# A hybrid block on one core: gates' stores in written order on GpSimd, the copy of inverse row sums between two row maxima, and the first gated rows' sums one tile later

## Chip, core and metric

The kernel runs on one core of one Trainium2 chip. The metric is the device time of one execution in microseconds (us), as the median of several runs; lower is better. A core has TensorE (PE, the matmuls), VectorE (DVE), ScalarE (ACT), GpSimd (POOL) and SyncE (SP). Each runs its own instructions one after the other, and they meet at semaphores. Transfers between the device memory and the on-chip memory go through DMA queues. Here SP and GpSimd issue them: SP's are in the queue that the profile calls q1 and GpSimd's in q0. Matmul results land in PSUM banks, out of which DVE or ACT must move them before a bank is used again.

## What is computed

The reference is one layer of a residual block on x of 1024 rows by 1024 columns, in float32:

```python
def mixer(h, w_in, b_f, conv_w, w_branch, w_out):
    proj = jnp.einsum("bsd,dn->bsn", h, w_in)
    q, k, v, f_logit, g_b, g_c, hc, gate_conv, gate_attn = jnp.split(proj, _SPLITS, axis=-1)
    ya = g_b * causal_depthwise_conv(g_c * hc, conv_w)
    logf = jax.nn.log_sigmoid(f_logit + b_f)
    yb = forgetting_attention(q, k, v, logf)      # 8 heads of 64, causal, blocks of 128 queries
    ya_d = jnp.einsum("bsc,cd->bsd", ya, w_branch[0])
    yb_d = jnp.einsum("bsc,cd->bsd", yb, w_branch[1])
    merged = jax.nn.sigmoid(gate_conv) * ya_d + jax.nn.sigmoid(gate_attn) * yb_d
    return jnp.einsum("bsd,de->bse", merged, w_out)

def swiglu(h, w_gate_up, w_down):
    g, u = jnp.split(jnp.einsum("bsd,df->bsf", h, w_gate_up), 2, axis=-1)
    return jnp.einsum("bsf,fd->bsd", jax.nn.silu(g) * u, w_down)

h = rmsnorm(x, norm_mix_pre);  x = x + rmsnorm(mixer(h, ...), norm_mix_post)
h = rmsnorm(x, norm_ffn_pre);  x = x + rmsnorm(swiglu(h, ...), norm_ffn_post)
```

The FFN has 2816 hidden columns. The attention's softmax is divided at the end by its row sums, of which the kernel forms the inverses.

## The kernel before

**Products.** The large products are cut into two by two blocks and done with seven block products in place of eight (Strassen's scheme in Winograd's form). For that, sums S1 to S4 of the blocks of one factor and T1 to T4 of the other are formed beforehand, and the block products are added up afterwards in the accumulators `c11`, `c12`, `c21` and `c22`. Every float32 operand is cut into a high and a low part (`hi` and `lo`, names such as `hT12h` and `hT12l`), and a block product is three matmuls: low times high, high times low, high times high. In the projection and the FFN DVE and ACT cut up the weights ("raw" tiles, loaded by SP) a tile ahead of PE, DVE also adds the products up (`c<-c,b`), and ACT drains some banks.

**Order.** All instructions go through a wrapper (lines 65 to 79). An engine that is named in `strict[0]` gets its instruction pinned behind the one that was written just before it on that engine. An instruction that is not pinned is placed by the scheduler: among those that are ready by its reckoning, the one written earlier goes first. Pinning fixes the order of issue alone; the waits for data are the same.

**The projection.** Eighteen jobs run one after the other: 0 to 3 for q and k, then the parts of the short convolution, and 10 to 17 for the gates. Each is one `strassen` call of some 84 matmuls. A gate job ends with the sigmoids of its four accumulators on ACT and four stores of 256 KB to `sg_dram` by GpSimd (lines 1291 to 1295). In the job 17, the last, the attention has already begun, its order is wholly written out (`last_pair`), and no sigmoid is taken. Beside the jobs, other work is spread in small steps over the additions of the `strassen` calls (table `plans`): the operands of the branch product (`ya_steps`, which loads `rows` from `ya_dram`, and stores blocks to `ya_ops`) and of the output product (`wo_steps`, which loads `r` and `l` from `w_out` and stores to `wt_dram`). These steps are pinned on DVE and GpSimd.

**The attention.** Twenty-one steps t; in each PE forms the scores of up to two blocks of rows for a pair of heads, DVE takes the row maximum of each head (`row_max`, which also writes the scores into the on-chip memory), ACT the exponentials, and PE the products with v. All engines are in written order here. At the steps 8, 13, 17 and 19 `inverse_rows` takes the inverse of a pair's row sums on DVE (`ri`), transposes it on PE (`tr`), and returns a function, `turned`, which copies the transpose (`rT<-tr`, DVE), stores it to the device memory and has SP load it back spread over the partitions. The step loop calls `turned` behind the row maxima of the first group; at t = 17, the third pair's, it calls it ahead of them (lines 1641 to 1643).

**The FFN.** Twenty-two hidden tiles of 128 columns, f = 0 to 21, each one `strassen` call. The first product of the first ten is formed ahead, so such a tile takes PE about 13.6 us; f = 2 stands at about 757.6 to 771.2 us and f = 3 up to 785. A tile ends with the gated rows `yf` (`um<-sgf,c`, DVE), two halves of one slot of `um`. For the down product their Winograd sums are formed from two tiles at a time by the generator `y_sums(k)`, k = f // 2. Its first half stores A12 and A22 and forms and stores S1 and S3; its second forms and stores S2 and S4 (`um<-um` on DVE, one `a_dram` store each on GpSimd). Before the change the first half runs at an odd f, the second at the next f (lines 2286 to 2291). The sums and their stores aren't pinned.

## Time and profile before

| what | us |
|---|---|
| median of 3 runs | 1310.73 (1310.16 to 1311.96) |
| profiled execution | 1313.74 |
| its span, first to last instruction | 1312.0 |
| TensorE busy | 1301.8 (99%), 6671 matmuls |
| VectorE busy | 948.5 (72%) |
| ScalarE busy | 564.0 (43%) |
| GpSimd busy | 207.8 (16%) |
| DMA | 235.64 MB, 180 GB/s on average |

The profile comes from one execution, whose time is 1.7 us longer than its span. Each line of a timeline names the start, the duration, the engine, the operation with the written tile, an arrow and the tiles read, and in square brackets how long the engine had been idle before and what ended that. Since nearly all instructions go through one helper, all have the line L76, and they are told apart by tiles. The stages stand in this order: the first norm and the start of the products with it up to about 63 us, the jobs of the projection to about 395, the attention from there to about 550, the rest of the branch product, the output product and the first products of ten hidden tiles to about 730, the hidden tiles to about 1096, and the down product to the end.

### The profile page before, as it was taken

How to read it: one execution, taken by the hardware profiler on the slowest of the kernel's cores; microseconds unless marked ns; L12 is line 12 of the kernel's file. 1: busy time of each engine (PE TensorE's matmuls, PEld its weight loads, DVE VectorE, ACT ScalarE, POOL GpSimd, SP SyncE). 2: the span in 40 equal slices, each digit the busy share in tenths (PEclk: the TensorE clock that was granted, in tenths of full speed). 3: DMA queues.
4: the chain of work that ended last, by engine and by line, in shares of the span. 5: the costliest groups of instructions: out<-in, count | busy, mean ns of one | idle time of the engine just before them, and what ended most of it. 6: DMA issues, size and time to landing. Idle time of an engine off the chain costs nothing.

```text
span 1312.0 us, 17799 instructions
## 1 busy us (share of the span) xinstructions
PE 1301.8 (99%) x6671; PEld 1084.2 (83%) x6671; DVE 948.5 (72%) x1361; ACT 564.0 (43%) x880; POOL 207.8 (16%) x375
## 2 busy tenths in 40 slices
PE   9999999999999999999999999999999999999998
PEld 8988888888788888888888878888888888888886
DVE  6877778776666678887677688866766666676675
ACT  6633333243355766423778332322232234444451
POOL 4101111112122222101232122111100110000000
PEclk9999999999999999999999999999999999999999
DMA  6355535557557566875486565533323337965551
GB/s 223 91 162 186 182 130 176 163 191 236 196 198 255 181 221 201 264 257 176 123 239 216 168 207 184 185 106 105 113 72 120 104 115 273 365 210 193 160 169 64
DMA packets 179639, 235.64 MB, mean 180 GB/s; under 512 B 12233, under 2 KB 121873, under 8 KB 179041
## 3 DMA queue, kind: packets, MB, share of 16 engines
q1 hardware_dynamic: 153392, 146.11, 35.5%
q0 software_dynamic: 26144, 88.40, 18.7%
q8 instruction: 52, 0.85, 0.3%
q14 instruction: 35, 0.28, 0.1%
q10 hardware_dynamic: 16, 0.00, 0.0%
HBM read 164.94 MB, written 69.53 MB: 179 GB/s over the span
## 4 chain that ended last, share of the span: by engine, by line
PE 95%; DVE 2%; DMA 2%; issue 1%; ACT 0%; SPq 0%; DVEq 0%; POOLq 0%; POOL 0%; ACTq 0%
PE b L76 60%; PE pd L76 16%; PE pv L76 4%; PE pbb L76 3%; PE pba L76 3%; PE po L76 3%; PE tps L76 3%; PE sp L76 2%; PE tp L76 1%; PE ma L76 1%; DMA raw<-in_w_in_dram 1%; PE mb L76 1%; DMA raw<-in_w_gate_up_dram 1%; DMA xt<-in_x_dram 0%; DVE c L76 0%
## 5 line engine op out<-in xcount | busy, mean ns | idle before, releaser
L76 DVE TENSOR_TENSOR c<-c,b 128x512 f32<-128x512 f32 x215 | 146.6, 683 | 72.9 <-PE b L76 70.8
L76 DVE TENSOR_TENSOR lo<-raw,hi 128x1024 fp32r<-128x1024 f32 (+1 forms) x91 | 109.7, 1205 | 73.5 <-PE b L76 57.0
L76 ACT ACTIVATE hi<-raw 128x1024 fp32r<-128x1024 f32 (+1 forms) x98 | 99.6, 1016 | 93.5 <-PE b L76 49.2
L76 ACT ACTIVATE hi<-sx 128x1024 fp32r<-128x1024 f32 x44 | 46.7, 1062 | 185.5 <-PE b L76 160.7
L76 DVE TENSOR_TENSOR lo<-sx,hi 128x1024 fp32r<-128x1024 f32 x44 | 53.8, 1223 | 38.9 <-PE b L76 37.7
L76 PE MATMUL b<-w12h,lo 128*128 128x512 f32 x208 | 80.9, 389 | 0.0
L76 DVE TENSOR_TENSOR sx<-raw 128x512 f32<-128x512 f32 x78 | 53.7, 688 | 36.9 <-DMA raw<-in_w_in_dram 25.6
L76 PE MATMUL b<-w12h,hi 128*128 128x512 f32 x204 | 79.4, 389 | 0.0
L76 PE MATMUL b<-w12l,hi 128*128 128x512 f32 x204 | 79.4, 389 | 0.0
L76 PE MATMUL b<-hh,hi 128*128 128x512 f32 x176 | 68.9, 392 | 0.5 <-DVE c L76 0.5
L76 PE MATMUL b<-hl,hi 128*128 128x512 f32 x176 | 68.5, 389 | 0.0
L76 PE MATMUL b<-hh,lo 128*128 128x512 f32 x176 | 68.5, 389 | 0.0
L76 PE MATMUL b<-w,s4h 128*128 128x512 f32 x208 | 64.1, 389 | 0.0
L76 POOL DMA_DIRECT2D a_dramA<-um x33 | 17.9, 543 | 287.4 <-DVE um L76 286.9
L76 PE MATMUL pd<-hi,lo 128*128 128x512 f32 x160 | 62.3, 389 | 0.0
L76 PE MATMUL pd<-hi 128*128 128x512 f32 x160 | 61.9, 390 | 0.0
L76 PE MATMUL pd<-ghi 128*128 128x512 f32 x148 | 57.6, 389 | 0.0
L76 PE MATMUL pd<-glo,ghi 128*128 128x512 f32 x148 | 57.6, 389 | 0.0
L76 PE MATMUL pd<-ghi,glo 128*128 128x512 f32 x148 | 57.6, 389 | 0.0
L76 PE MATMUL b<-hT12h,lo 128*128 128x512 f32 x136 | 53.0, 390 | 1.6 <-DVE lo L76 1.6
L76 ACT ACTIVATE sgf<-c 128x512 f32<-128x512 f32 x32 | 20.3, 633 | 77.8 <-DVE c L76 60.2
L76 PE MATMUL b<-hT34h,hi 128*128 128x512 f32 x136 | 53.0, 390 | 0.0
(492 smaller groups left out, 3637.7 us busy)
## 6 DMA issues: line engine op xcount, KB each, us to landing
raw<-in_w_gate_up_dram SPq DMA_DIRECT2D x52, 512.0 KB, 3.9
raw<-in_w_in_dram SPq DMA_DIRECT2D x35, 512.0 KB, 5.7
a_dramS<-um POOLq DMA_DIRECT2D x44, 256.0 KB, 3.0
a_dramA<-um POOLq DMA_DIRECT2D x33, 256.0 KB, 2.4
sg<-sg_dram SPq DMA_DIRECT2D x32, 256.0 KB, 5.5
graw<-a_dramS SPq DMA_DIRECT2D x14, 512.0 KB, 3.9
sg_dram<-c POOLq DMA_DIRECT2D x24, 256.0 KB, 2.4
raw<-in_w_down_dram SPq DMA_DIRECT2D x11, 512.0 KB, 6.0
```

What stands on the lines that cost most here:

```text
L76: ins = getattr(self.engine, name)(*args, **kw)
```

## The change

It has three parts, which touch three stages.

1. **Gate jobs** (from line 1294): GpSimd is named in `strict[0]` while the four `sg_dram` stores of a gate job are written, so they take their written place between the pinned steps of the branch and output operands. The last two are written in the other order, `c22` before `c21`.
2. **Attention, step 17** (lines 1641 to 1643): the early call of `turned` is taken out. The call behind the row maxima of the first group, which all other steps use, now copies the third pair's inverse rows as well. The first group of step 17 has one row block of one head, so the copy stands between the row maxima of the block's first head and its second.
3. **FFN** (lines 2286 to 2291): `y_sums(0)` runs its first half at f = 2 (before: f = 1) and its second at f = 3 (before: f = 2), where it stands ahead of the first half of `y_sums(1)`. The other sums stay.

```diff
                 for t in (c12, c21, c22):
                     nc.scalar.activation(t, t, AF.Sigmoid)
-            for r, c, t in ((0, n1, so), (0, n2, c12), (1, n1, c21), (1, n2, c22)):
+            strict[0] = ("gpsimd",)
+            for r, c, t in ((0, n1, so), (0, n2, c12), (1, n2, c22), (1, n1, c21)):
                 nc.gpsimd.dma_start(sg_dram[j][r, :, c], t)
+            strict[0] = ()
...
         if t <= 5:
             po_copy = pv_pair(t - 2)
-        if turned and t == 17:
-            turned()
-            turned = None
         for i, e in now[0]:
             row_max(t, i, e)
...
         if f % 2:
             late_sums = y_sums(f // 2)
+        if f == 2:
+            first_sums = late_sums
+            next(first_sums)
+        if f == 3:
+            next(first_sums)
+        if f % 2 and f > 1:
             next(late_sums)
-        else:
+        if f % 2 == 0:
             nc.gpsimd.dma_start(a_dram["A11"][f // 4][f // 2 % 2], yf[:, n1])
-        if f and (f % 2 == 0 or f == NF - 1):
+        if f > 2 and (f % 2 == 0 or f == NF - 1):
             next(late_sums)
```

## The prediction, made before the changed kernel was run

> **What bounds the kernel now.** First the page: its head and its chain of waits by engine.

> ```profile
> span 1312.0 us, 17799 instructions
> PE 1301.8 (99%) x6671; PEld 1084.2 (83%) x6671; DVE 948.5 (72%) x1361; ACT 564.0 (43%) x880; POOL 207.8 (16%) x375
> PE 95%; DVE 2%; DMA 2%; issue 1%; ACT 0%; SPq 0%; DVEq 0%; POOLq 0%; POOL 0%; ACTq 0%
> ```

> TensorE is busy for 99% of the span. The change takes no matmul away, so its gain can come only out of places where PE stands still. Next the waits of PE, and three pieces of the chain of waits in order of time.

> ```profile
> PE b L76 <- DVE lo L76: 1.6, 1, 1.6
> ...
> PE b L76 <- DVE c L76: 0.5, 1, 0.5
> PE sp L76 <- DVE nm L76: 0.3, 1, 0.3
> ...
> 323.18 9.67 DMA raw<-in_w_in_dram
> 763.11 6.60 DMA raw<-in_w_gate_up_dram
> 777.33 318.73 PE b L76 x1404
> ```

> The three waits shown are one event each, and each lies beside one part of the diff; the two left out are at the start of the kernel, before any of it. The last row gives the undisturbed pitch: 318.73 / 1404 = 0.227 us from the start of one matmul to the next. Shown idle time counts from a modelled end, so I price a stall as start to start minus the usual pitch.

> **Stall A (part 1's neighbourhood).** PE, then DVE, in the timeline:

> ```profile
> 335.51 0.39 PE L76 MATMUL b<-hT12l,hi 128*128 128x512 f32 x1
> 337.51 0.50 PE L76 MATMUL b<-hT12h,lo 128*128 128x512 f32 x1 [1.60 <-DVE lo L76]
> 332.97 0.69 DVE L76 TENSOR_TENSOR sx<-raw 128x512 f32<-128x512 f32 x1 [6.47 <-DMA raw<-in_w_in_dram]
> 336.23 1.22 DVE L76 TENSOR_TENSOR lo<-raw,hi 128x1024 fp32r<-128x1024 f32 x1
> ```

> 337.51 - 335.51 - 0.227 = 1.77 us lost. The raw weights, issued by SP at 323.18, land 9.67 us later (332.85). DVE has waited 6.47 us and then needs until 337.45 to cut the operand that PE wants. Had the transfer taken 7.9 us (332.85 - 1.77 = 331.08), nothing would be lost; each us later costs one.

> **Stall B (part 2).**

> ```profile
> 513.66 0.47 PE L76 MATMUL sp<-hi 64*128 64x448 f32 x1
> 514.43 0.44 PE L76 MATMUL sp<-hi 64*128 64x448 f32 x1 [0.30 <-DVE nm L76]
> 510.61 0.25 DVE L76 RECIPROCAL ri<-rsum 128x16 f32<-128x16 f32 x1
> 511.72 0.28 DVE L76 COPY rT<-tr 16x128 f32<-16x128 f32 x1 [0.86 <-PE tr L76]
> 511.93 1.20 DVE L76 CUSTOM_DVE_ANT_0 pt<-sp,rows 128x1024 f32<-128x1024 f32 x1
> 513.07 1.21 DVE L76 CUSTOM_DVE_ANT_0 pt<-sp,rows 128x1024 f32<-128x1024 f32 x1
> ```

> 514.43 - 513.66 = 0.77, less one pitch: 0.55 us lost. The score matmul at 514.43 needs the bank that the second row maxima read until 514.28. Both maxima stand behind the copy `rT<-tr`, which waits 0.86 us for a transpose.

> **Stall C (part 3).**

> ```profile
> 776.48 0.39 PE L76 MATMUL b<-w12h,lo 128*128 128x512 f32 x1
> 777.33 0.50 PE L76 MATMUL b<-hh,hi 128*128 128x512 f32 x1 [0.46 <-DVE c L76]
> 758.79 0.68 DVE L76 TENSOR_TENSOR um<-um 128x512 f32<-128x512 f32 x1
> 765.41 0.69 DVE L76 TENSOR_TENSOR um<-um 128x512 f32<-128x512 f32 x1
> 769.80 0.69 DVE L76 TENSOR_TENSOR sx<-raw 128x512 f32<-128x512 f32 x1 [1.95 <-DMA raw<-in_w_gate_up_dram]
> 776.60 0.68 DVE L76 TENSOR_TENSOR c<-c,b 128x512 f32<-128x512 f32 x1
> ```

> 777.33 - 776.48 - 0.227 = 0.62 us lost: the add at 776.60, which frees a bank, stands in a backlog that DVE has had since its 1.95 us wait for the raw weights at 769.80. The three `um<-um` between 758.79 and 765.41 (first and last quoted) are the sums S1, S2 and S4 of the first gated rows.

> The three stalls together are 2.94 us, 0.22% of the time. What this kernel's measurement can tell from no change is about 0.2%, 2.6 us: even all three gone would show only just.

> **The change, part by part.**

> *Part 2, the copy between two maxima.* It removes and adds no instruction. The first maxima can start where the reciprocal ends, at 510.61 + 0.25, about 510.87, and run into the time in which DVE waited. They end near 512.05; the copy, whose transpose was done at 511.72, follows, and the second maxima begin about 512.25 and end about 513.45, ahead of the score matmul's place (about 513.87). So DVE's wait of 0.86 us goes and stall B with it: -0.55. What moves besides: the copy's DMAs, the store of the inverse and SP's loads back, come 0.3 us later and serve a division steps later. Next late there is nothing: DVE is 0.83 us earlier. Bounds: 0 (if something else on DVE fills the gap) and -0.55.

> *Part 3, the sums one tile later.* Same four sums, same four `um` stores and the stores of A12 and A22; S1 and S3 go from f=1 to f=2, S2 and S4 to f=3. Each sum costs DVE 0.6 us from start to start (758.79 to the next instruction). Two of the three, S1 and S2, stand ahead of the subtraction that frees the raw buffer; its load goes out at 763.11 and takes 6.60 us. With 2 x 0.6 = 1.2 us less ahead of it the load goes out at about 761.9 and lands about 768.5; the backlog starts 1.2 us earlier, the add comes at 775.4, and PE, due at 776.71, does not wait: -0.62. The price is paid one tile on, where two sums of the first pair and two of the second meet. There S2 and S4 of the first pair, 2 x 0.6 = 1.2 us, come on top of S1 and S3 of the second. Their cover is the time in which DVE waits for PE in the tile after the stall, in the table by windows (us, then busy time of PE, PEld, DVE, ACT and POOL):

> ```profile
> 785.60:799.20 13.60, 13.60 (x62) 11.26 (x61) 11.53 (x17) 4.03 (x5) 3.78 (x7) 1.00 0.68 224
> ```

> 13.60 - 11.53 = 2.07 us are free there, more than 1.2. The stores move on GpSimd's queue only, 1.5 MB of them a tile later, and their readers are the down products, tiles later. These sums are not pinned, so the scheduler may also leave one where it was. Bounds -0.73 (the slower next pitch included) and +0.5 (the sums push the next tile's add as far as these did); taken -0.6.

> *Part 1, the gates' stores in written order.* No bytes change: four stores of 256 KB per gate job, each about 0.55 us of GpSimd. What changes is what they stand behind. GpSimd before, in the timeline, jobs 12 and 13:

> ```profile
> 309.14 0.55 POOL L76 DMA_DIRECT2D rows<-ya_dram  x1
> 312.15 0.54 POOL L76 DMA_DIRECT2D rows<-ya_dram  x1
> 314.60 0.54 POOL L76 DMA_DIRECT2D sg_dram<-c  x1 [1.91 <-ACT c L76]
> 322.24 0.72 POOL L76 DMA_DIRECT2D ya_ops<-yh  x1 [2.57 <-issue]
> 327.58 0.56 POOL L76 DMA_DIRECT2D sg_dram<-c  x1 [2.99 <-ACT c L76]
> ```

> The row at 314.60 was the last of job 12's four stores. Now these wait behind the pinned stores of the branch operand, two of 0.7 us whose data come about when that row went, so all four go at about 316 to 318. The two `rows` loads are written behind the stores and pinned, so they no longer go at 309.14 and 312.15 but near 319. That is 2 MB (4 x 256 KB and 2 x 512 KB) taken out of the stretch up to 315 and put into 316 to 332, the flight of the raw load that makes stall A. Against it one store (327.58) leaves that flight, 0.25 MB. What the load meets there is in the DMA views of 326 to 330 and of 330 to 332:

> ```profile
> q0 software_dynamic: 308, 1.13, 76.2%
> q1 hardware_dynamic: 296, 0.15, 18.3%
> ...
> q1 hardware_dynamic: 735, 0.37, 61.2%
> q0 software_dynamic: 109, 0.33, 41.0%
> ```

> While GpSimd's queue (q0) is full, SP's (q1, where the raw load is) moves 0.15 MB in 4 us, 38 KB/us; as q0 runs dry, 0.37 MB in 2 us, 185 KB/us. The 512 KB load thus ends about when q0 has drained. By total rate, (1.13 + 0.15) / 4 = 0.32 MB/us, 1.75 MB more would take 5.5 us more; but GpSimd issues the later traffic of that stretch later too (322.24 already waited 2.57 us to be issued), so that part of it falls behind 332, when the load is through. Bounds: -1.77 (the store at 327.58 and what slips are enough for the load to land by 331.08) and +5 (q0 full until the raw load has crept through). I take a fifth of the upper way, nearest to the row that shows q0 draining at 330 with 2 MB more in front and some 1.5 MB slipping behind: the load 0.7 us later, +0.7.

> [...]

> Two more places. Job 15's stores now all precede the two `wt_dram` stores behind which ACT waits in the first row below, 0.75 MB or, at 0.32 MB/us, 2.3 us more ahead of `wt_dram<-h`:

> ```profile
> 385.00 1.06 ACT L76 ACTIVATE h<-l 128x1024 fp32r<-128x1024 f32 x1 [2.73 <-DVE lo L76]
> 391.88 0.60 ACT L76 ACTIVATE c<-ma 128x512 f32<-128x512 f32 x1
> 394.35 0.39 PE L76 MATMUL ma<-hT12h,hi 128*128 128x512 f32 x1
> 411.90 0.88 POOL L76 TENSOR_TENSOR yb<-rows,mask 128x128 f32<-128x128 f32 x2
> 415.95 0.28 DVE L76 CUSTOM_DVE_ANT_0 rows<-sp,yb 128x128 f32<-128x128 f32 x1
> ```

> ACT overwrites `h` at 385.00, after that store has read it, and works through to the eviction that ends at 392.48, 1.87 us ahead of the matmul that needs the bank: at worst 2.3 - 1.87 = 0.4 us, taken 0. And job 17's four stores, 4 x 0.55 = 2.2 us, now stand ahead of the mask work at 411.90; waiting their turn they push it to about 415.2, its end to 416.05, 0.1 us into DVE's read at 415.95. DVE is not what PE waits for there: 0, at worst 0.2.

> **Sum** against the profiled execution, 1313.74 us (span 1312.0 and 1.74 around it): +0.7 - 0.55 - 0.6 = -0.45. The profiled execution is 3.0 us above the median of the runs shown (1310.73), so the forecast is that median less 0.45, 1310.3.

> **Rivals.**
> 1. *All three stalls go.* If less of the branch traffic meets the raw load, -1.77 - 0.55 - 0.62 = -2.94: 1307.8. For it: the load needs to be only 1.77 us quicker, and one 256 KB store leaves. Against it: 2 MB move towards it. Chance 0.17.
> 2. *Slower: the raw load starves.* One mechanism at 326 to 338: if q0 is never empty until the load is through, it moves its 512 KB at 38 KB/us from 326 on, with 0.06 MB or so landed before, to about 338, +5 and more; +5 - 1.15 = +3.85: 1314.6. It decides from a landing of about 334.1 on (+1.2, where the gains of parts 2 and 3 are used up), and shows as slower from 336.6 on. For it: the packets row above. Against it: GpSimd itself is held up by its waits to issue, which spaces the traffic. Chance 0.11.
> 3. *The reordering does not do what it says*: the sums, unpinned, stay at 758 to 765 and the load lands as before; only part 2 counts, -0.55: 1310.2. Chance 0.22, and not to be told from the forecast by the time alone.

> **How the numbers follow.** The forecast's case (part 1 between -1 and +3, parts 2 and 3 mostly won) has 0.50. Cases 3 and the forecast lie within 0.2% (1308.1 to 1313.35), 0.72 together. Rival 1 at 1307.8 is just over the line; a quarter of it stays within, so faster is 0.15 with 0.02 of other luck; slower is rival 2, 0.11, and 0.02 for the attention's start; same 0.72. The range goes from rival 1 with 0.2 to spare, 1307.6, to a landing 2.9 us above the forecast's, 1313.2; it leaves out rival 2 and a little of rival 1.

> **What would show it.** Stall B: the wait of `sp` for `nm` gone from PE's waits, the copy between two maxima near 512.0. Stall C: the wait on `c` at 777 gone, the raw load out by 762, and three or four `um<-um` behind 771. Part 1: in the timeline of GpSimd the `rows` loads near 319, the raw load issued at 323.18 landing between 332 and 335, and `b` still waiting for `lo` by 1 to 4 us. I am wrong if that load lands by 331, if it lands after 336, or if a wait stands at 394 or 416 that was not there.

## The result, and the profile after

The changed kernel took 1317.23 us (median of 6 runs, 1316.07 to 1319.53), the kernel before 1310.10 us beside it (6 runs, 1309.92 to 1311.96). The ratio is 1.0053, with a 95% interval of 1.0040 to 1.0066: 7 us slower, where 0.5 us faster was forecast, and above the range. The profiled execution of the changed kernel took 1317.19 us with a span of 1315.4 us.

First the waits of PE in the changed kernel (in total, times, longest, us):

```profile
PE b L76 <- DVE lo L76: 3.0, 1, 3.0
PE spin L76 <- DVE zero L76: 1.4, 1, 1.4
PE b L76 <- DVE c L76: 0.5, 1, 0.5
...
PE pba L76 <- DVE yB L76: 0.2, 1, 0.2
```

Stall B (`sp` for `nm`) is gone. Stall A has grown from 1.6 to 3.0 us. A wait for `c` of the size of stall C is still there, and the wait of `pba` for `yB` is new. Both kernels run the same 6671 matmuls, in the same order but for two that the scheduler set ahead of 36 others near 763 to 772, so the loss can be placed: take a matmul's start in the changed kernel less the start of the same matmul before, and see where this difference steps.

| place (time before) | the difference steps by | what is there |
|---|---|---|
| up to 12 us | -1.87 | the start; full clock was granted from 11.2 us on in the profiled execution of before (a `spin` matmul took 0.41 us at 9.6 and 0.28 at 11.6), from 5.2 us on in this one; no part of the change is there |
| 337.5 | +1.37 | stall A longer |
| 337.5 to 345 | +2.79 | matmuls at half clock |
| 394 to 400 | +0.67 | the matmuls on `ma` and `mb` |
| 418 | +0.87 | `pba<-yB` |
| 514 | -0.74 | stall B gone |
| 762 to 771 | +1.26 | new stalls in the FFN tile f = 2 |
| 775 to 786 | -0.95 | stall C gone |

At the last matmul the difference is 3.47 us; without the start it would be 5.3.

**Stall A.** The piece of the chain with the load, then DVE, then PE:

```profile
321.40 11.04 DMA raw<-in_w_in_dram
...
332.56 0.69 DVE L76 TENSOR_TENSOR sx<-raw 128x512 f32<-128x512 f32 x1 [7.84 <-DMA raw<-in_w_in_dram]
...
333.74 0.39 PE L76 MATMUL b<-hT12l,hi 128*128 128x512 f32 x1
337.09 0.80 PE L76 MATMUL b<-hT12h,lo 128*128 128x512 f32 x1 [2.97 <-DVE lo L76]
337.69 0.63 PE L76 MATMUL b<-hT12h,hi 128*128 128x512 f32 x1
338.11 0.63 PE L76 MATMUL b<-hT12l,hi 128*128 128x512 f32 x1
```

The raw load now takes 11.04 us (9.67 before), and the stall is 337.09 - 333.74 - 0.227 = 3.12 us. Then comes what the forecast did not have: from 337.69 the matmuls follow each other at 0.43 us in place of 0.227. The table by windows (us, busy time of PE, PEld, DVE, ACT, POOL, then the granted clock, DMA share, GB/s) names it:

```profile
333.00:337.05 4.05, 1.12 (x5) 0.58 (x4) 3.98 (x7) 1.68 (x3) 1.09 (x2) 0.91 0.07 30
337.05:341.00 3.95, 3.91 (x9) 3.17 (x10) 3.33 (x6) 1.64 (x3) 0.54 (x1) 0.50 0.98 289
341.00:345.00 4.00, 4.00 (x14) 3.17 (x14) 1.64 (x3) 2.00 (x2) 0.00 (x0) 0.73 0.65 195
```

PE is busy in the second row and does 9 matmuls in the time of 17: its granted clock is 0.50. A busy PE is not a fast one, and the waits don't show this loss at all.

**What the load meets.** GpSimd in the timeline, then the DMA view of 323 to 331, and last GpSimd's queue over the whole flight of the load, before (323.2 to 332.85) and in the changed kernel (321.4 to 332.4):

```profile
314.30 0.55 POOL L76 DMA_DIRECT2D sg_dram<-so  x1
...
316.76 0.54 POOL L76 DMA_DIRECT2D rows<-ya_dram  x1
317.71 0.54 POOL L76 DMA_DIRECT2D rows<-ya_dram  x1 [0.40 <-issue]
...
324.02 0.55 POOL L76 DMA_DIRECT2D l<-in_w_out_dram  x1 [2.24 <-issue]
...
q0 software_dynamic: 760, 2.74, 86.1%
q1 hardware_dynamic: 738, 0.38, 16.5%
...
q0 software_dynamic: 601, 2.13, 62.1%
q0 software_dynamic: 878, 3.14, 73.4%
```

Job 12's stores and the `rows` loads stand where the forecast put them (316.76 is 318.5 on the clock of before). In these 8 us of the flight GpSimd's queue moves 2.74 MB, and the raw load's queue 0.38 MB in nearly as many packets, 47 KB/us. Over the whole flight GpSimd's queue moves 3.14 MB, 1.0 MB more than before.

### The profile page after: what moved, and what is told of

The parts are those of the page before. It is cut to its first block, busy times and chain, and to the rows that moved or that the text cites. A ratio compares the mean times of both kernels' runs of the same rounds, so it can differ in the third digit from the quotient of the medians.

```text
span 1315.4 us, 17789 instructions
## 1 busy us (share of the span) xinstructions
PE 1303.2 (99%) x6671; PEld 1083.5 (82%) x6671; DVE 949.7 (72%) x1361; ACT 564.4 (43%) x880; POOL 207.7 (16%) x375
## 4 chain that ended last, share of the span: by engine, by line
PE 96%; DMA 2%; DVE 1%; issue 1%; ACT 0%; DVEq 0%; POOLq 0%; POOL 0%; ACTq 0%
PE b L76 60%; PE pd L76 16%; PE pv L76 3%; PE pbb L76 3%; PE pba L76 3%; PE tps L76 3%; PE po L76 2%; PE sp L76 2%; PE tp L76 1%; PE ma L76 1%; DMA raw<-in_w_in_dram 1%; DMA raw<-in_w_gate_up_dram 1%; PE mb L76 0%; DVE lo L76 0%; DVE sx L76 0%
## 5 line engine op out<-in xcount | busy, mean ns | idle before, releaser
L76 DVE TENSOR_TENSOR c<-c,b 128x512 f32<-128x512 f32 x215 | 146.6, 682 | 79.9 <-PE b L76 74.3
L76 DVE TENSOR_TENSOR lo<-raw,hi 128x1024 fp32r<-128x1024 f32 (+1 forms) x91 | 109.6, 1204 | 76.2 <-PE b L76 60.3
L76 ACT ACTIVATE hi<-raw 128x1024 fp32r<-128x1024 f32 (+1 forms) x98 | 99.6, 1016 | 95.3 <-PE b L76 49.4
L76 ACT ACTIVATE hi<-sx 128x1024 fp32r<-128x1024 f32 x44 | 46.7, 1062 | 199.5 <-PE b L76 171.5
L76 DVE TENSOR_TENSOR lo<-sx,hi 128x1024 fp32r<-128x1024 f32 x44 | 53.8, 1223 | 40.0 <-PE b L76 38.8
L76 PE MATMUL b<-w12h,lo 128*128 128x512 f32 x208 | 80.9, 389 | 0.0
L76 PE MATMUL b<-w12h,hi 128*128 128x512 f32 x204 | 79.4, 389 | 0.0
L76 PE MATMUL b<-w12l,hi 128*128 128x512 f32 x204 | 79.4, 389 | 0.0
L76 DVE TENSOR_TENSOR sx<-raw 128x512 f32<-128x512 f32 x78 | 53.6, 688 | 31.5 <-DMA raw<-in_w_in_dram 22.2
L76 PE MATMUL b<-hh,hi 128*128 128x512 f32 x176 | 69.0, 392 | 0.6 <-DVE c L76 0.5
L76 PE MATMUL b<-hh,lo 128*128 128x512 f32 x176 | 68.5, 389 | 0.0
L76 PE MATMUL b<-hl,hi 128*128 128x512 f32 x176 | 68.5, 389 | 0.0
L76 PE MATMUL b<-w,s4h 128*128 128x512 f32 x208 | 64.0, 389 | 0.0
L76 POOL DMA_DIRECT2D a_dramA<-um x33 | 17.9, 543 | 287.4 <-DVE um L76 287.0
L76 PE MATMUL pd<-hi,lo 128*128 128x512 f32 x160 | 62.2, 389 | 0.0
L76 PE MATMUL pd<-hi 128*128 128x512 f32 x160 | 61.9, 390 | 0.0
L76 PE MATMUL pd<-ghi 128*128 128x512 f32 x148 | 57.6, 389 | 0.0
L76 PE MATMUL pd<-glo,ghi 128*128 128x512 f32 x148 | 57.6, 389 | 0.0
L76 PE MATMUL pd<-ghi,glo 128*128 128x512 f32 x148 | 57.6, 389 | 0.0
L76 PE MATMUL b<-hT12h,lo 128*128 128x512 f32 x136 | 54.0, 397 | 3.0 <-DVE lo L76 3.0
L76 PE MATMUL b<-hT12h,hi 128*128 128x512 f32 x136 | 53.6, 394 | 0.0
L76 PE MATMUL b<-hT12l,hi 128*128 128x512 f32 x136 | 53.6, 394 | 0.0
## 6 DMA issues: line engine op xcount, KB each, us to landing
raw<-in_w_gate_up_dram SPq DMA_DIRECT2D x52, 512.0 KB, 4.0
raw<-in_w_in_dram SPq DMA_DIRECT2D x35, 512.0 KB, 5.7
graw<-a_dramS SPq DMA_DIRECT2D x14, 512.0 KB, 3.9
raw<-in_w_down_dram SPq DMA_DIRECT2D x11, 512.0 KB, 5.7
```

Of the source, the lines that this page charges most:

```text
L76: ins = getattr(self.engine, name)(*args, **kw)
```

## The experiments

Each kernel is given against the kernel before, run beside it on the same chip. The first theory, P, is that part 1 is the loss, by the load's flight, the half clock behind the stall, and smaller stalls at 394 and 418. Its rivals stand in the expectations.

### The three parts apart

Part 1 alone, parts 2 and 3 without it, part 2 alone and part 3 alone; each has the hunks of the diff above that belong to it.

> Only part 1 (gate stores in written order). Theory P: the whole loss is part 1: the raw load lands 1.6 us later, and the longer stall costs another 2.6 us of half clock behind it, 0.9 at the matmuls on ma/mb and 0.8 where the masks lie beside a DVE subtraction: 5 to 7 us above before, and a window behind the stall with a granted clock near 0.5. Rival Q: the loss comes from part 3's other order in the FFN or from the execution: within 1.5 us of before.

> Parts 2 and 3 without part 1. Theory P: about -0.2 us against before (part 2 -0.5, part 3 +0.1 to +0.4 since its stall only moves one tile ahead), no half clock anywhere. Rival Q: 3 us or more above before.

> Only part 2 (the copy between two maxima). Theory P: the 0.55 us wait of sp for nm at step 17 gone, time -0.3 to -0.6 us. Rival: something else at that place takes the gain, 0.0.

> Only part 3 (the sums one tile later). Theory P: the wait on c near 777 gone, a like one about 8 us ahead of it in its place, net 0 to +0.5 us. Rival (my forecast's step): -0.6 us.

| kernel | median, us (runs) | before, us | ratio, 95% interval |
|---|---|---|---|
| part 1 alone | 1317.06 (5) | 1311.44 (27) | 1.0050, 1.0036 to 1.0063 |
| parts 2 and 3 | 1311.40 (11) | 1311.44 | 1.0000, 0.9991 to 1.0010 |
| part 2 alone | 1310.98 (11) | 1311.44 | 0.9993, 0.9982 to 1.0005 |
| part 3 alone | 1312.46 (11) | 1311.44 | 1.0006, 0.9998 to 1.0015 |

Part 1 is the loss; Q falls. In the profile of part 2 alone the wait of `sp` for `nm` is gone, and the matmuls step 0.74 us closer there, as in the seven other profiles with part 2 (0.73 to 0.74). DVE in the changed kernel has the copy between the two maxima, without a wait:

```profile
514.68 1.16 DVE L76 CUSTOM_DVE_ANT_0 pt<-sp,rows 128x1024 f32<-128x1024 f32 x1
...
515.76 0.27 DVE L76 COPY rT<-tr 16x128 f32<-16x128 f32 x1
515.97 1.20 DVE L76 CUSTOM_DVE_ANT_0 pt<-sp,rows 128x1024 f32<-128x1024 f32 x1
```

So the copy does what was forecast, though so small a gain is inside the interval. Part 1 alone kept its full clock in the profiled execution (1.00 from 333 to 345), against the expectation, with a stall of 3.33 us; that execution, 1314.29 us, was the shortest of its five. Nor did it lose anything at 394, where P put 0.9 us.

Part 3 behaves as P has it in kind, at a higher price than its 0.5 us. In the changed kernel, DVE and PE in the timeline:

```profile
768.09 0.68 DVE L76 TENSOR_TENSOR um<-um 128x512 f32<-128x512 f32 x1
770.23 0.69 DVE L76 TENSOR_TENSOR sx<-raw 128x512 f32<-128x512 f32 x1 [1.45 <-DMA raw<-in_w_gate_up_dram]
770.84 0.68 DVE L76 TENSOR_TENSOR um<-um 128x512 f32<-128x512 f32 x1
771.44 1.22 DVE L76 TENSOR_TENSOR lo<-raw,hi 128x1024 fp32r<-128x1024 f32 x1
772.57 0.68 DVE L76 TENSOR_TENSOR c<-c,b 128x512 f32<-128x512 f32 x1
...
773.31 0.50 PE L76 MATMUL b<-hh,hi 128*128 128x512 f32 x1 [0.50 <-DVE c L76]
```

The raw load went out and landed earlier, as forecast (770.23 is about 767.0 on the clock of before, where it was 769.80). But the scheduler, which places the unpinned instructions, set `sx<-raw` of the next tile, which waits for it, ahead of `lo<-raw` and of the add at 772.57, which frees the bank for this tile's last product. Before, those two ran at 766.03 and 767.17, ahead of the wait. So stall C left 777 and came back three products (36 matmuls) earlier, at 773.31. About a third of the new loss, 0.45 of the 1.26 us, stands still earlier, from 767.03 on, behind the two matmuls that the scheduler set ahead; the profile names no wait for it. Together the new loss is 1.15 to 1.55 us in the six profiles with part 3, 1.35 on average; the old one, which is gone in all of them, took 0.03 to 0.94 in the twelve without, 0.43 on average. Part 3 so costs 0.9 us against the usual execution, and 1.0 us in the medians. S2 and S4 also still run at 768.09 and 770.84, in f = 2: written one tile later, they weren't executed a tile later.

### Which gate jobs

Part 1 for some of the jobs only; the other stores as before.

```diff
+            strict[0] = ("gpsimd",) if ij < 14 else ()     # and: in (14, 15); > 15; != 12; == 12
+            order = ((0, n1, so), (0, n2, c12), (1, n1, c21), (1, n2, c22))
+            if strict[0]:
+                order = order[:2] + order[:1:-1]
+            for r, c, t in order:
```

> Part 1 only for the gate jobs 10 to 13; the later stores unpinned as before. Theory P: the raw load issued near 322 still takes 11 us, the stall near 337 is 3.3 us, and in most executions half clock follows it for 2.6 us: 4.5 to 6 us above before. Rival R (the loss sits in the later jobs and the start of the attention): within 1.5 us of before.

> Part 1 only for jobs 14 and 15. Theory P: the store of h behind job 15's stores may reach ACT late, the matmuls on ma wait 0 to 0.9 us, no stall over 2 us near 337: 0 to +0.9 us. Rival R: +2 us or more.

> Part 1 only for jobs 16 and 17. Theory P: job 17's four stores push the mask work on GpSimd onto DVE's subtraction yB<-yraw,yB, which then takes 2.2 us in place of 1.5, and the pba matmuls wait: +0.7 us. Rival R: +2 us or more; rival S: the mask work lies beside nothing that PE waits for, 0.

> Part 1 for every gate job but 12: job 12's stores and the two rows loads stand in the order of before, all else as in part 1 alone. Theory P (the 2 MB moved at job 12 meet the raw load): flight of the raw load 5 to 9.7 us as in the kernels without part 1, stall 0 to 1.8 us, no half clock; +0.7 us stays from jobs 16 and 17: 1311 to 1312. Rival U (job 13's stores, moved too, delay it): flight 11 us and 1316 to 1317.

> Part 1 for job 12 alone (its four stores, and behind them the two rows loads). Theory P (job 12 is the whole of it): the raw load takes about 11 us, stall 3.3 us, median 5 to 6 us above before. Rival W (it takes job 13's stores as well): 2 us or less.

| part 1 for | median, us (runs) | before, us | ratio, 95% interval |
|---|---|---|---|
| jobs 10 to 13 | 1316.83 (5) | 1310.82 (23) | 1.0040, 1.0026 to 1.0053 |
| jobs 14 and 15 | 1311.11 (12) | 1310.82 | 1.0003, 0.9992 to 1.0015 |
| jobs 16 and 17 | 1311.58 (11) | 1310.82 | 1.0007, 0.9997 to 1.0016 |
| all but job 12 | 1311.81 (11) | 1310.81 (35) | 1.0008, 0.9998 to 1.0017 |
| job 12 alone | 1315.92 (7) | 1311.69 (19) | 1.0030, 1.0019 to 1.0042 |

Job 12 is enough for the long stall and its clock, and without it they are gone; R, U and W fall. Job 12 alone costs 4.2 us in the medians, less than the 5 to 6 that P gave it. For job 12 alone, PE in the timeline and two windows:

```profile
334.76 0.39 PE L76 MATMUL b<-hT12l,hi 128*128 128x512 f32 x1
338.51 0.69 PE L76 MATMUL b<-hT12h,lo 128*128 128x512 f32 x1 [3.36 <-DVE lo L76]
...
337.00:339.00 2.00, 0.49 (x1) 0.40 (x2) 2.00 (x4) 1.58 (x2) 1.10 (x2) 0.91 0.34 133
339.00:341.00 2.00, 2.00 (x6) 1.61 (x5) 1.42 (x4) 1.11 (x2) 0.54 (x1) 0.50 0.91 237
```

With jobs 16 and 17 alone PE loses 0.91 us near 418 (0.7 was expected), as in every kernel with these jobs in written order (0.87 to 0.91 us, none in the others). DVE and GpSimd there:

```profile
413.10 2.18 DVE L76 TENSOR_TENSOR yB<-yraw,yB 128x1024 fp32r<-128x1024 f32 x1
...
413.10 0.45 POOL L76 TENSOR_TENSOR yb<-rows,mask 128x128 f32<-128x128 f32 x1
413.50 0.28 POOL L76 COPY yb<-rows 128x128 f32<-128x128 f32 x1
413.75 0.45 POOL L76 TENSOR_TENSOR yb<-rows,mask 128x128 f32<-128x128 f32 x1
414.16 1.43 POOL L76 TENSOR_TENSOR rows<-rows,mask 128x128 f32<-128x128 f32 x1
```

And before, the same subtraction, the one mask beside it, and the next subtraction of the same form:

```profile
416.16 1.50 DVE L76 TENSOR_TENSOR yB<-yraw,yB 128x1024 fp32r<-128x1024 f32 x1
416.12 0.45 POOL L76 TENSOR_TENSOR rows<-rows,mask 128x128 f32<-128x128 f32 x1 [1.11 <-DVE nm L76]
...
421.70 1.22 DVE L76 TENSOR_TENSOR yB<-yraw,yB 128x1024 fp32r<-128x1024 f32 x1
```

Before, all mask work but one instruction was done when the subtraction started; it took 1.50 us, and 1.22 with no mask beside it. Beside four instructions of the mask work DVE takes 2.18 us, and the last mask 1.43 in place of 0.46. Side by side both engines' instructions grow, DVE's by 0.96 us and the mask by 0.97; how they hold each other up, no run here shows. In time, 0.8 us is inside the interval; S is refuted by the profiles. With jobs 14 and 15 alone PE loses nothing at 394; P had allowed 0 to 0.9 us there.

### What in job 12's move delays the load

The two `rows` loads of job 12 (1 MB) one step earlier, with part 1 alone; and the two loads of `w_out` rows (1 MB, issued by GpSimd at about the time of the raw load) one job later, with the whole change.

```diff
+        if k == 0:
+            strict[0] = ("gpsimd",)
+            load_rows(ya_rows(1), nc.gpsimd)
+            strict[0] = ()
         spill(ya_ops, 0, k, t, staged())
         yield
-        if k == 0:
-            strict[0] = ("gpsimd",)
-            load_rows(ya_rows(1), nc.gpsimd)
-            strict[0] = ()
```

```diff
-        (((13, 1), (15, 0), (16, 0), (16, 1)), lambda: wo_steps(3)),
+        (((14, 1), (15, 0), (16, 0), (16, 1)), lambda: wo_steps(3)),
```

> Part 1 alone with the two rows loads of job 12 (1 MB) written one step earlier, ahead of the two branch stores, where the GpSimd queue is idle. Theory P1 (the loads and job 12's stores weigh alike, a MB each): the raw load takes 7 to 9 us, stall 0 to 1.2 us, 1311 to 1313. Rival P2 (the stores alone are enough): 11 us and 1316.

> The changed kernel with the two loads of w_out rows (r and l, 1 MB), which GpSimd issues just behind the raw load, one job later, behind the branch stores of job 14. Theory P: with 1 MB less on GpSimd's queue the raw load takes 6 to 8 us, no stall near 337, no half clock: 1311 to 1312.5, unless the moved loads meet the raw load of 344, which has 1 to 4 us of slack. Rival V (the raw load is late for a reason of its own, not for GpSimd's bytes): 11 us, 1317.

With the `rows` loads early: 1313.78 us (12 runs, before 1310.81), ratio 1.0017, 1.0008 to 1.0025; the stall is 1.71 us with full clock. That is above P1's range in time, flight and stall, and 2.2 us below P2's time: neither has the size. With the `w_out` loads later: 1315.98 us (11 runs), ratio 1.0030, 1.0021 to 1.0040; the stall near 337 is 0.22 us, but the time is far above P's 1311 to 1312.5, since the moved loads made a new stall, on PE:

```profile
364.49 0.39 PE L76 MATMUL b<-hB22h,s4l 128*128 128x512 f32 x1
367.06 0.79 PE L76 MATMUL b<-hT34h,hi 128*128 128x512 f32 x1 [2.18 <-DVE c L76]
367.65 0.63 PE L76 MATMUL b<-hT34l,hi 128*128 128x512 f32 x1
...
362.92 0.43 DVE L76 CAST h<-l 128x512 fp32r<-128x512 f32 x1 [2.21 <-DMA sg_dram<-so]
```

DVE's work on these rows is pinned; its first instruction stands in front of the adds, 2.21 us late, and PE pays 2.34 us, then half clock again (0.50 from 367 to 369). That instruction reads `l`, one of the two moved loads: issued at 355.25, it took 7.6 us, to 362.9. The row names a store that was in flight with it. So V falls (the raw load does come earlier with fewer bytes beside it, 8.2 us of flight with 2.1 MB against 11.2 with 3.1), and the same bytes elsewhere met another deadline.

Over all the profiles the picture is one of dose. The flight here is from the issue of the raw load to DVE's first instruction on it; the next column is what GpSimd's queue moved meanwhile (a longer flight also takes in more); the stall is start to start less 0.227 us, and what PE lost at half clock behind it is counted in the same way.

| kernel | flight, us | GpSimd's queue, MB | stall, us | lost at half clock, us |
|---|---|---|---|---|
| before | 9.8 | 2.1 | 1.77 | 0.1 |
| part 2 alone | 8.2 | 1.7 | 0.20 | 0.1 |
| part 3 alone | 5.2 | 0.7 | 0 | 0 |
| parts 2 and 3 | 9.0 | 2.1 | 0.98 | 0.1 |
| part 1, jobs 14 and 15; jobs 16 and 17 | 5.3; 5.4 | 0.7; 0.7 | 0; 0 | 0; 0 |
| part 1, all but job 12 | 9.1 | 1.9 | 1.08 | 0.1 |
| part 1, `rows` loads early | 9.7 | 2.3 | 1.71 | 0.1 |
| the change, `w_out` loads later | 8.2 | 2.1 | 0.22 | 0.1 |
| part 1 alone | 11.4 | 3.1 | 3.33 | 0.1 |
| part 1, jobs 10 to 13; job 12 alone | 11.6; 11.6 | 3.2; 3.1 | 3.52; 3.52 | 1.7; 1.7 |
| the change; once more | 11.2; 11.7 | 3.1; 3.1 | 3.13; 3.66 | 2.9; 2.6 |

The first seven profiles (four rows, then three kernels in two) have job 12 as before. In six of them the instructions at this place are the same (in the seventh the stores of jobs 10, 11 and 13 are pinned), and yet the flights go from 5.2 to 9.8 us and the stalls from 0 to 1.77 us, on average over the seven 0.58. The 1.77 us of the profile of before is the worst of the seven. What tells them apart is a race of two engines: where GpSimd issues the first `w_out` load (`r`) behind SP's raw load, by 0.08 to 0.33 us, the flight is 5.2 to 5.4 us (three profiles); where it does so ahead, by 0.07 to 1.95 us, the flight is 8.2 to 9.8 us (four). No run sets this order by itself; with both `w_out` loads moved away ("A version that beats both") the flight is 5.1 and 6.2 us. With job 12 moved and nothing else done about it the five stalls average 3.43 us, 2.85 more, and the half clock 1.8.

### The clock behind the stall

Matmuls that compute nothing of use, into the bank that the waiting product's first matmul overwrites: the operand comes when it comes, but PE is idle for less.

```diff
+        for _ in range(warm_up):      # in job 14: 8 with part 1 alone, 12 with the whole change
+            nc.tensor.matmul(
+                b3, w["S1"][0][:, 0, :], hb[T1][0][:, 0, :], start=True, stop=True
+            )
         prod(b3, w["S1"], hb[T1], True)
```

> Part 1 alone, and in job 14 eight more matmuls of 0.227 us ahead of the product that waits, into the bank which its first matmul overwrites. The load lands as late as with part 1 alone, so PE's result is needed at the same time, but PE is idle 1.8 us less. Theory P (the long idle time lets the clock fall): granted clock 1.00 behind the stall in the profile, and a median near 1314.3, 2 to 3 us below part 1 alone. Rival T (the clock falls for another reason, or seldom matters): half clock in some executions as before, median as for part 1 alone, 1317.

> The changed kernel once more, for the comparison in the same call: about 1317, a stall of about 3.3 us near 337, half clock behind it or not.

> The changed kernel with 12 more matmuls (2.7 us) in the bank of the product that waits: the operand comes at the same time, PE is idle for under 1 us. Theory C (the idle time near 337 lets the clock fall, and that is 2.6 us in most executions): 1.5 to 2.6 us below after_again, clock 1.00. Rival D (the half clock is rare or cheap; the load itself lands later in most executions than in the profiled ones): less than 0.8 us below after_again.

Eight of them with part 1 alone: 1316.17 us (5 runs), ratio 1.0037, 1.0024 to 1.0049, granted clock 1.00 behind the stall. The time lies between P's 1314.3 and T's 1317, and the clock was full in the profile of part 1 alone as well, so this run decides nothing. Twelve with the whole change: 1316.56 us (6 runs), 1.0036, 1.0022 to 1.0050; the change once more, beside it: 1317.86 us (5 runs), 1.0049, 1.0035 to 1.0062. Of these two kernels one window each, first the change, then with the twelve:

```profile
339.00:341.00 2.00, 2.00 (x6) 1.60 (x5) 1.42 (x3) 1.06 (x2) 0.54 (x1) 0.50 0.86 226
```

```profile
339.00:341.00 2.00, 2.00 (x11) 1.65 (x10) 1.82 (x3) 0.11 (x1) 0.54 (x1) 1.00 1.08 306
```

With PE kept busy the clock is full, where the change has half clock in both of its profiles, and the load is as late as ever (flight 11.0 us). That is one profile with the twelve; that the idle time is what lets the clock fall is inferred from it and from where the clock fell in five of the eighteen profiles (last section). In time the two kernels differ by 1.3 us, between what C and D expected, and their intervals overlap; both theories are left standing there. The runs of one kernel lie up to 5 us apart (1314.66 to 1319.71 with the twelve), and of runs without a profile only span and mean clock are known, so what else differs between them isn't known.

### A version that beats both

Part 2, and the two `w_out` loads moved out of the raw load's way: one job later, or one job earlier, where GpSimd's queue has room. No part 1, no part 3.

```diff
-        (((13, 1), (15, 0), (16, 0), (16, 1)), lambda: wo_steps(3)),
+        (((12, 0), (15, 0), (16, 0), (16, 1)), lambda: wo_steps(3)),
```

> The kernel before with part 2 and with the same two loads one job later; no part 1, no part 3. Theory P: the raw load takes about 5 us in every execution, so the stall near 337, which before shows in some executions only, is gone, and the copy's 0.55 us too: 0.6 to 1.5 us below before (1309.5). Rival: the moved loads stall the raw load of 344 or wt_dram: not below before.

> The kernel before with part 2 and with the two loads of w_out rows one job earlier, where GpSimd's queue is idle for part of the time, in place of behind the raw load. If the raw load then takes 5 us in every execution: 0.7 to 1.5 us below before. Rival: the loads wait on GpSimd for their buffers and hold up job 12's stores and the rows loads behind them: same as before or up to 3 us slower.

Later: 1310.25 us (12 runs, before 1310.81), 0.9995, 0.9987 to 1.0003, not to be told from before; the stall near 337 is gone, and PE loses 0.97 us near 367. Earlier: 1310.08 us (11 runs, before 1311.69), ratio 0.9986, 0.9978 to 0.9995. That is faster than before by 1.6 us in the medians (by the interval 0.7 to 2.9 us), and so than the changed kernel. GpSimd in its timeline:

```profile
291.05 0.54 POOL L76 DMA_DIRECT2D r<-in_w_out_dram  x1
...
301.08 0.54 POOL L76 DMA_DIRECT2D l<-in_w_out_dram  x1 [2.75 <-DMA wt_dram<-l]
304.42 0.56 POOL L76 DMA_DIRECT2D sg_dram<-so  x1 [2.81 <-ACT so L76]
```

The second load does wait for its buffer (2.75 us), as the rival had it, but the store behind it then waits for ACT another 2.81 us, so that store isn't held up. The flight of the raw load is 6.2 us, the stall 0.

## Why the prediction was wrong

**The step that failed** is the size of part 1: "the load 0.7 us later, +0.7". Its mechanism was right, and so were its places: the stores at 316 to 318, the `rows` loads near 319, a landing between 332 and 335, `b` waiting for `lo` by 1 to 4 us, all came as written. What the term measured, against the profile of before: the stall longer by 1.37 us (1.89 when the change was run once more), and behind it 2.4 to 2.8 us at half clock, for which the sum had no term. Two errors made it small. "GpSimd issues the later traffic of that stretch later too" was taken to put 1.5 of the moved 2 MB behind the load. That left about 0.25 MB more in the flight (2 less 1.5 less the store that goes). GpSimd was held up (2.24 us at 324.02), but its queue moved 1.0 MB more in the flight (3.14 against 2.13) and was still busy up to about 330.5. And "each later us costs one" holds only as long as the clock does.

**The base.** The working was made against one execution with a stall of 1.77 us, and its sum was then taken off the median of the runs. A stall that varies between executions can't be carried over so. On average it was 0.58 us in the seven profiles with job 12 as before, and the same holds for stall C, 0.43 on average where the forecast took 0.62 to 0.73 from the one profile (0.94 there by the count used here). Made against these averages, the sum closes, all in us:

| kernel | stall A | half clock | 394 | 418 | part 2 | part 3 | sum | medians apart |
|---|---|---|---|---|---|---|---|---|
| the change (its two profiles) | 2.8 | 2.7 | 0.4 | 0.9 | -0.7 | 0.9 | 7.0 | 7.1 and 6.2 |
| part 1 alone | 2.85 | 1.8 | 0 | 0.9 | | | 5.5 | 5.6 |
| part 1, job 12 alone | 2.85 | 1.8 | | | | | 4.6 | 4.2 |
| part 1, jobs 10 to 13 | 2.85 | 1.8 | | | | | 4.6 | 6.0 |
| part 3 alone | | | | | | 0.9 | 0.9 | 1.0 |
| part 2 alone | | | | | -0.7 | | -0.7 | -0.5 |

For the three kernels with part 1 or a piece of it that moves job 12 stall and clock are the averages of the five profiles with a long stall. The medians are known to about 1.5 us, so the table shows that nothing large is missing, not each size.

**Part 2** was right: -0.55 was forecast, and 0.74 us less stands in every profile with it. Its time alone can't be told from no change.

**Part 3** was forecast at -0.6 and costs 0.9. The step "the backlog starts 1.2 us earlier, the add comes at 775.4, and PE ... does not wait" came true for that add. What failed was to treat DVE's order as kept: the sums aren't pinned, and the scheduler moved the wait for the raw load ahead of an add that had been done before it. Rival 3 was half right: S2 and S4 stayed in f = 2, and S3 in f = 1 (749.63, which is 746.4 on the clock of before, where it ran at 746.45). S1, S2 and S4 ran 1.9 to 4.3 us later, all still in f = 2.

**The smaller places.** At 394, 0.4 us was allowed at worst and 0 taken; ACT got `h` late, and PE lost 0.67 us in the first profile of the change and 0.12 in the second. This loss varies: of the nine profiles with job 15's stores in written order four have it, 0.12 to 0.75 us, and of the nine others none. The row at 385.00 that the forecast quoted waited for DVE's `lo`, not for the store; in the first profile of the change the same instruction waits for the store:

```profile
390.95 1.07 ACT L76 ACTIVATE h<-l 128x1024 fp32r<-128x1024 f32 x1 [4.02 <-DMA wt_dram<-h]
```

At 418, 0.2 was the worst and 0.9 came, since the mask work was laid beside the DVE read but not beside the subtraction behind it.

**The rivals.** Rival 2, the starving load, was the case that came, at 1314.6 forecast against 1317.2, with a chance of 0.11. The load landed at 334.2 and 334.7 in the two profiles, on the clock of before. That is past the 334.1 from which this rival was to decide, and short of the 336.6 from which it was to show as slower. The rest was the half clock, and gains that were not there to be had. This rival's sum, made with the raw load at 38 KB/us beside GpSimd's full queue (47 KB/us was measured in 323 to 331), was nearer than the forecast.

## What to carry to other kernels

Here a load in packets of 0.5 KB with a deadline was delayed by the traffic in packets of 3.6 KB that shared its flight: 5.2 us with 0.7 MB of it, 11.2 to 11.7 us with 3.1 to 3.2 MB. The two queues moved nearly as many packets (738 beside 760 in 8 us); whether they take turns by packets is not shown, since no run changed the packet sizes. Before pinning stores "in order", add up the bytes that the pinning moves into each such flight, since instructions pinned behind them move too. A stall that leaves PE idle for some 2 us (2.01 to 3.27 us ahead of the falls here) should be priced with the clock that may fall in it (1.7 to 2.9 us near 337), and the profile's granted clock read right behind each long wait. And a stall in one profile is a sample: look at it in two or three profiles before it is taken as the gain to be had.

## What was not expected of the hardware

So each trace can be cut into pieces of 3.413 us from a change of its clock on, and PE's idle time added up in each. In the five profiles in which the clock fell between the start and the last matmul, the piece that ends at the fall had 2.01 to 3.27 us of idle time. Of the other pieces none had more than 1.61 us in the profile of before and 0.75 us in that of the changed kernel, and behind none of them did the clock fall. The stall of 3.33 us that cost no clock has 3.17 us of idle time, from 334.53 to 337.70. By an estimate, which carries the 3.413 us on in that trace from the first change of its clock, an edge at 336.35 cuts this into 1.82 and 1.34 us; then what such a stall costs here depends on where it falls. Where between 1.82 and 2.01 us the limit would lie, and whether it is the same in other kernels, no run here shows.
